# mLSTM branch operands by token chunks, the last gate unit's chunks in turns, and ada units moved ahead, in a one-core encoder step

## The chip, the core and the metric

The kernel runs on one core of a Trainium2 chip. The metric is the device time of one execution in microseconds, of which several runs are taken. The engines are named as in the profile: PE (TensorE matmul), PEld (its weight loads), DVE (VectorE), ACT (ScalarE), POOL (GpSimd), SP (SyncE, which here issues most DMAs).

## The reference, cut to what matters

One layer of an encoder for 1024 prompt tokens and one group of 64 sample tokens, so T = 1088 tokens, D_MODEL = 1024. Two branches, attention `y_a` and mLSTM `y_b`, are each projected to D_MODEL, weighted by sigmoid gates computed from the input, and summed.

```
mod = jax.nn.silu(c) @ w_ada + b_ada
sh1, sc1, g1, sh2, sc2, g2 = jnp.split(mod[:, None, :], 6, axis=-1)
u = _rmsnorm(x, norm1_g) * (1 + sc1) + sh1
proj = u @ w_in
sq, sk, sv, mqk_pre, mv, mo, mi, mf, ga, gb = jnp.split(proj, idx, axis=-1)
...
y_a = _stick_breaking(sq.reshape(B, L, SB_HEADS, SB_HEAD_DIM), k_all, v_all, q_start)
...
h, C1, n1, m1 = _mlstm(mq, mk, mvh, log_i, log_f, C0, n0, m0)
...
y_b = jax.nn.sigmoid(mo) * h
merged = jax.nn.sigmoid(ga) * (y_a @ w_a) + jax.nn.sigmoid(gb) * (y_b @ w_b)
x = x + g1 * (merged @ w_out)
u2 = _rmsnorm(x, norm2_g) * (1 + sc2) + sh2
x = x + g2 * ((jax.nn.silu(u2 @ w_ff_gate) * (u2 @ w_ff_up)) @ w_ff_down)
```

Attention has 8 heads of 64. For each block of 128 queries it takes the scores z, their sigmoid, a running product along the keys (as a scan), and the weighted sum of the values.

## The kernel before, in words

Everything is float32, and nearly every projection is made of three matmuls on operands split into a high and a low part (`mm3`, L75: high × high, high × low, low × high). Activations lie transposed, features on the 128 partitions and the 1088 tokens along the free axis, in three token chunks `CHUNKS` of 320, 384 and 384. A weight unit is 512 KB: its raw tile (`wr`, 3 buffers) is loaded from SP's queue, and POOL makes the high and the low tile out of it (`wh`, `wl`, 3 buffers each; L53 and L59).

The kernel is built by a scheduler that fixes the order of the instructions on each engine at build time: it reads the code as a list, and lets later work go ahead where it reckons an engine free. On the chip each engine then keeps that order, and waits on semaphores.

The part that the change touches is the phase "at", about 500 to 897 us of the profile. There four pairs of heads go through attention. `run(attention(p), chain(fill), 27, 0)` (L854) lists the whole of attention of pair p and behind it the dense filler; the scheduler weaves the filler in among attention's chains, which go from PE (scores, `z`, L526 and L527) over DVE (mask L388), ACT (sigmoid L392, `be` L393), DVE (scan L396, product `be` L397), back to PE (transposes into `ps_a`, L540), ACT and DVE (split into `ah` and `al`, L47 and L56), PE (`po`, L547), ACT and DVE (`yo`, `ya`, L553 and L554). Names read so: `be_3_0_5` is pair 3, head 0, query block 5.

The filler of pairs 0 to 2 is 14 gate units and 22 ada units. A gate unit (`gate_unit`, `unit` L346) projects the input (operands `uh`, `ul`, 8 feature blocks each) to 128 gate columns: for each chunk 24 matmuls over the 8 feature blocks kb into one PSUM bank, a sigmoid on ACT (L825), and a store from SP to `ga_d` or `gb_d`. `gb7` is the last of them, and the last reader of `uh` and `ul`. An ada unit (`ada_unit`, `ada_blocks` L213) loads 512 KB of w_ada into a `wr` buffer and makes 128 columns of the modulation: 16 small matmuls (L223), a copy on DVE (L226), a transpose on PE (L228), a sum and an addition on DVE (L233, L235).

The filler of pair 3 is 8 ada units (40 to 47) and then `branch_b` (L982): the mLSTM branch's projection by w_b. Its operands `yh4` to `yh7` and `yl4` to `yl7` lie ready split in DRAM (`yb_d`), and are loaded into the 16 buffers that held `uh` and `ul` (`load_y` with b of 4 or more, L963). Each of its 8 output blocks m takes the three chunks in turn: 12 matmuls into one of two banks (`cur["d"]` is 2), a load of the gate chunk `lgb` (L995), a copy on ACT (`tb`, L997), a multiply on POOL (L998), and a store to `pb_d` (L999). At m of 2, 3 and 4 it also loads attention's results of pairs 0 to 2 (`load_y(0)` to `load_y(2)`) and POOL splits them into `yh0` to `yl2`. The merge with w_a follows from 897 us, then w_out and the feed-forward part.

Of the kernel before, what the change touches and what calls it, by code (L numbers as in the profile page):

```python
# [8 lines left out]
F32 = mybir.dt.float32  # L9
# [5 lines left out]
P = 128  # L15
# [4 lines left out]
KB = 8  # L20
EPS = 1e-6
CHUNKS = [(0, 320), (320, 704), (704, 1088)]
# [13 lines left out]
def trunk(ctx, tc, a, o, dbg=None, stop=None):  # L36
    nc = tc.nc
# [14 lines left out]
    def hi_pool(out, in_):  # L52
        nc.gpsimd.tensor_scalar(out, in_, 1.0, 0.0, ALU.mult, ALU.add)  # L53
# [4 lines left out]
    def lo_pool(out, in_, h):  # L58
        nc.gpsimd.tensor_sub(out, in_, h.bitcast(F32))  # L59

    def w_unit(fills, name):
        raw = wp.tile([P, KB, P], F32, tag="wr", name=f"wr_{name}")
        for dst, src in fills(raw):
            nc.sync.dma_start(dst, src)
        wh = wp.tile([P, KB, P], F32R, tag="wh", name=f"wh_{name}")
        wl = wp.tile([P, KB, P], F32R, tag="wl", name=f"wl_{name}")
        hi_pool(wh, raw)
        lo_pool(wl, raw, wh)
        return wh, wl

    def cols(w, c0, n=P):

        return w[:, c0 : c0 + n].rearrange("(kb p) n -> p kb n", p=P)

    def mm3(ps, wh, wl, xh, xl, first, last):  # L75
        nc.tensor.matmul(ps, wh, xh, start=first, stop=False)  # L76
        nc.tensor.matmul(ps, wh, xl, start=False, stop=False)
        nc.tensor.matmul(ps, wl, xh, start=False, stop=last)
# [14 lines left out]
    w_a, w_b, w_out = a["w_a"][0], a["w_b"][0], a["w_out"][0]  # L93
# [50 lines left out]
    yb_d = dram.tile([4, 2, P, T], F32, name="yb_d")  # L144
# [37 lines left out]
    def small(shape, name, tag, dtype=F32, bufs=2, pool=None):  # L182
        return (pool or cur["sb"]).tile(shape, dtype, tag=tag, name=name, bufs=bufs)
# [11 lines left out]
    def bank(tag, name, bufs=2):  # L195
        return cur["ps"].tile([P, 512], F32, tag=tag, name=name, bufs=bufs)

    cur = {}
# [40 lines left out]
    uh, ul = [], []  # L239
# [11 lines left out]
    c0 = small([16, P], "c0", "c0", bufs=1)  # L251
# [91 lines left out]
    def evac_v(p, ps, s, e):  # L343
        nc.scalar.copy(pairs[p].vf[:, s:e], ps[:, : e - s])

    def unit(name, fills, evac, alloc=None):  # L346
        wh, wl = w_unit(fills, name)
        if alloc:
            alloc()
        for c, (s, e) in enumerate(CHUNKS):  # L350
            ps = bank("d", f"ps_{name}_{c}", cur["d"])
            for kb in range(KB):
                mm3(ps[:, : e - s], wh[:, kb, :], wl[:, kb, :], uh[kb][:, s:e], ul[kb][:, s:e], kb == 0, kb == KB - 1)
            evac(ps, s, e)
            yield

    def w_cols(c0):
        return lambda raw: [(raw, cols(w_in, c0))]
# [463 lines left out]
    def gate_unit(b, c0, dst, name):  # L822
        def fin(ps, s, e):
            t = small([P, 384], f"gt_{name}{b}_{s}", "gt", bufs=cur["gt"])
            nc.scalar.activation(t[:, : e - s], ps[:, : e - s], AF.Sigmoid)  # L825
            nc.sync.dma_start(dst[b][:, s:e], t[:, : e - s])
        return unit(f"{name}{b}", w_cols(c0 + b * P), fin)

    def in_unit(name, c0, i, evac, alloc):
        return unit(name, w_cols(c0), lambda ps, s, e: evac(*i, ps, s, e), lambda: alloc(*i))  # L830
# [12 lines left out]
    def ada_unit(i):  # L843
        ada_blocks((i,), "d", cur["d"], lambda i: wp.tile([P, KB, P], F32, tag="wr", name=f"wada{i}"))
        if 32 <= i < 40:
            b = i - 32
            nc.vector.tensor_scalar(A2[:, b, :], mod[:, i, :], 1.0, n2g(b), ALU.add, ALU.mult)
        yield

    def chain(gens):  # L850
        for g in gens:
            yield from g

    def run(consumer, dense, nsteps, nd):  # L854

        n = 0.0
        done = False
        if nd == 0:
            for _ in consumer:
                pass  # L860
            done = True
        for _ in dense:
            n += nsteps / max(nd, 1)
            while n >= 1.0 and not done:
                n -= 1.0
                done = next(consumer, "end") == "end"
        for _ in consumer:
            pass

    gates = [gate_unit(b, OFF_GA, ga_d, "ga") for b in range(KB)] + [gate_unit(b, OFF_GB, gb_d, "gb") for b in range(KB)]  # L870
    ada_left = [ada_unit(i) for i in range(16, 48)]
# [39 lines left out]
    for h in range(4):  # L911
        craw = small([P, P], f"c0_{h}", "S")
        nc.sync.dma_start(craw, a["state_mlstm_C"][0, 0, h])
        ps = bank("t", f"ps_c0{h}", 3)
# [24 lines left out]
    ps = bank("t", "ps_cvo", 3)  # L939
# [18 lines left out]
    yh, yl = {}, {}  # L958

    def y_tiles(b):  # L960
        yh[b] = up.tile([P, T], F32R, tag="u", name=f"yh{b}")
        yl[b] = up.tile([P, T], F32R, tag="u", name=f"yl{b}")

    def load_y(b):
        y_tiles(b)
        if b >= 4:
            for i, t in enumerate((yh[b], yl[b])):
                nc.sync.dma_start(t.bitcast(F32), yb_d[b - 4, i])
            return
        raw = up.tile([P, T], F32, tag="u", name=f"yr{b}")  # L970
        nc.sync.dma_start(raw, ya_d[b])
        for s, e in CHUNKS:
            hi_pool(yh[b][:, s:e], raw[:, s:e])
            lo_pool(yl[b][:, s:e], raw[:, s:e], yh[b][:, s:e])

    def wide_unit(w, r0, nb, q, name):

        ws = w_unit(lambda raw: [(raw.rearrange("p (k b) n -> p k (b n)", b=2)[:, :nb, :],
                                  w[r0 : r0 + nb * P, q * 256 : (q + 1) * 256].rearrange("(k p) n -> p k n", p=P))], name)
        return [x.rearrange("p (k b) n -> p k b n", b=2) for x in ws]  # L980

    def branch_b():  # L982

        for m in range(KB):
            if m % 2 == 0:
                wh, wl = wb0 if m == 0 else wide_unit(w_b, 0, 4, m // 2, f"wb{m}")
            if 2 <= m < 5:
                load_y(m - 2)
            for c, (s, e) in enumerate(CHUNKS):
                n = e - s  # L990
                ps = bank("d", f"ps_b{m}_{c}", cur["d"])
                for k in range(4):
                    mm3(ps[:, :n], wh[:, k, m % 2, :], wl[:, k, m % 2, :], yh[4 + k][:, s:e], yl[4 + k][:, s:e], k == 0, k == 3)
                gt = small([P, 384], f"lgb{m}_{c}", "gt", bufs=4)[:, :n]
                nc.sync.dma_start(gt, gb_d[m][:, s:e])  # L995
                t = small([P, 384], f"tb{m}_{c}", "gt", bufs=4)[:, :n]
                nc.scalar.copy(t, ps[:, :n])  # L997
                nc.gpsimd.tensor_mul(t, t, gt)  # L998
                nc.sync.dma_start(pb_d[m][:, s:e], t)  # L999
                yield  # L1000

    gi, ai = 2, 2
    for p, (ng, na) in enumerate(((5, 6), (5, 8), (4, 8))):
        gs, ads = gates[gi : gi + ng], ada_left[ai : ai + na]
        gi, ai = gi + ng, ai + na
        fill = []
        for i in range(na):
            fill += gs[i : i + 1] + ads[i * na // ng : (i + 1) * na // ng]
        run(attention(p), chain(fill), 27, 0)
    wb0 = wide_unit(w_b, 0, 4, 0, "wb0")  # L1010
    for b in range(4, 8):
        load_y(b)
    run(attention(3), chain(ada_left[24:32] + [branch_b()]), 27, 0)
    ph.close()


# [8 lines left out]
    def dbank(name):  # L1025
        return cur["p2"].tile([P, 512], F32, tag="d", name=name, bufs=6)
# [13 lines left out]
    for m in range(KB):  # L1040
        if m % 2 == 0:
            wh, wl = wide_unit(w_a, 0, 4, m // 2, f"wa{m}")
        for c, (s, e) in enumerate(CHUNKS):
# [6 lines left out]
            ps = dbank(f"ps_a{m}_{c}")  # L1050
# [224 lines left out]
    gb = gst.enter_context(tc.tile_pool(name="gb", bufs=8, space=PSUM, reuse_waits="tile"))  # L1275
# [243 lines left out]
    def add_x1(m, h, r, src):  # L1519

        if h is None:
            nc.vector.scalar_tensor_tensor(xq[m][:, :, r], src, gain(m, 0), xq[m][:, :, r], ALU.mult, ALU.add)
            return
        x = xq[m][:, h, r]
        for lo, hi, g in (by_group(0, QT) if h == r == 0 else [(0, QT, 0)]):
            nc.vector.scalar_tensor_tensor(x[:, lo:hi], src[:, lo:hi], gain(m, g), x[:, lo:hi], ALU.mult, ALU.add)
# [16 lines left out]
    def evac(p, m, h, ps):  # L1543
        if p == 5:
            add_x1(m, h, 1, ps)
        if p == 1:
            nc.scalar.copy(us[m][:, h], ps)
        elif p == 6:
            nc.vector.tensor_sub(us[m][:, h], us[m][:, h], ps)
            if h:  # L1550
                add_x1(m, None, 1, us[m])
                add_x1(m + 4, None, 1, us[m])
                for i in range(2):
                    add_x1(m + 4, i, 0, us[m][:, i])
        else:
            m_, r = {2: (m, 0), 5: (m + 4, 1), 3: (m, 1), 7: (m + 4, 1), 4: (m + 4, 0)}[p]
            add_x1(m_, h, r, ps)
            if p == 4:
                norm_step(m_, r, h)
            elif p != 5 and h:  # L1560
                norm_step(m_, r)
# [165 lines left out]
```

## Time and profile before

| | us |
|---|---|
| three runs | 1803.46, 1794.51, 1791.31 |
| median of the runs | 1794.51 |
| the profiled execution | 1791.73 |
| its span in the profile | 1790.0 |
| mean granted clock of PE | 0.988 |

The profile shows one execution; the times of its engines and stretches add up to its span, and a shift in them is set against 1791.73 us. The page's second part cuts the span into 40 slices of 44.75 us with the busy share in tenths (9 is 90% or more); the phase "at" is the twelfth to the twentieth of them:

```profile
PE   5899999999999999989998999999999999999998
```

A slice says little of what waits for what; for that the views by stretch and by wait are read, which the next sections quote.

### The profile page before, as it was taken

What the parts mean: (1) busy time and instruction counts of PE and PEld (TensorE: products, weight loads), DVE (VectorE), ACT (ScalarE), POOL (GpSimd) and SP (SyncE); (2) the same over time, 40 slices, a digit from 0 to 9 for tenths busy, and PEclk for the clock granted to TensorE, in tenths of its full rate; (3) what the DMA queues carried; (4) which work ended last, traced back from release to release, by engine and by line L of the source; (5) the groups of instructions that cost most, each with busy time, mean ns of one, the idle gap of its engine ahead of it and who ended that gap; (6) DMA issues with size and microseconds to landing.
All of it is one profiled execution on the core that took longest, in us unless ns stands there. A gap on an engine that the chain in (4) does not pass through costs nothing. (4 is left out here: it accounts for less than half of the span.)

```text
span 1790.0 us, 32786 instructions
## 1 busy us (share of the span) xinstructions
PE 1718.5 (96%) x12670; PEld 1656.9 (93%) x12670; DVE 1052.6 (59%) x2024; ACT 735.2 (41%) x1500; POOL 563.0 (31%) x507
## 2 busy tenths in 40 slices
PE   5899999999999999989998999999999999999998
PEld 4699999999988989877898999999999999999998
DVE  6623415152346858597554289666655677667965
ACT  5332333324233535353412367433333355453444
POOL 3434534545442232224877250044322100001000
PEclk9999999999999999999999999999999999999999
DMA  9426666664485565586576345744433488899852
GB/s 275 116 78 199 146 200 138 198 168 143 123 210 137 141 155 149 135 252 206 169 221 188 109 139 153 210 157 149 136 116 98 142 250 229 287 337 347 292 159 101
DMA packets 359533, 320.25 MB, mean 179 GB/s; under 512 B 16726, under 2 KB 327506, under 8 KB 359378
## 3 DMA queue, kind: packets, MB, share of 16 engines
q1 hardware_dynamic: 345074, 270.77, 50.2%
q0 software_dynamic: 14304, 47.39, 10.7%
q8 instruction: 100, 1.64, 0.4%
q14 instruction: 55, 0.45, 0.1%
HBM read 241.01 MB, written 98.09 MB: 189 GB/s over the span
## 5 line engine op out<-in xcount | busy, mean ns | idle before, releaser
L1609 PE MATMUL ps_d<-o,wh_d 128*128 128x272 f32 x1232 | 230.9, 287 | 0.2 <-DVE g L1370 0.2
L1609 PEld LDWEIGHTS ps_d<-o,wh_d 128*128 128x128 f32 x1232 | 192.9, 188 | 0.4 <-DVE g L1370 0.4
L1609 PE MATMUL ps_d<-o,wl_d 128*128 128x272 f32 x616 | 176.4, 288 | 0.0
L1609 PEld LDWEIGHTS ps_d<-o,wl_d 128*128 128x128 f32 x616 | 115.6, 188 | 0.0
L396 DVE TENSOR_TENSOR_SCAN re<-re 128x128 f32<-128x128 f32 (+3 forms) x64 | 105.8, 1654 | 14.3 <-ACT re L392 13.6
L47 ACT CAST w<-wr 128x512 fp32r<-128x512 f32 x140 | 85.0, 619 | 68.4 <-PE ps_gc L1382 27.1
L56 DVE TENSOR_TENSOR w<-wr,w 128x512 fp32r<-128x512 f32 x140 | 94.9, 691 | 21.4 <-ACT w L47 17.6
L1593 POOL DMA_DIRECT2D dsum_d<-wr_d x12 | 6.5, 538 | 237.9 <-DVE wr_d L1591 232.0
L392 ACT ACTIVATE re<-z 128x512 f32<-128x512 f32 (+2 forms) x96 | 47.5, 495 | 75.3 <-DVE z L388 55.4
L1382 PE MATMUL ps_ga<-b1h,w 128*128 128x272 f32 x352 | 74.6, 289 | 3.0 <-ACT g L1367 1.9
L1382 PE MATMUL ps_gc<-b5h,w 128*128 128x272 f32 x352 | 75.1, 293 | 0.0
L1382 PE MATMUL ps_gb<-b6h,w 128*128 128x272 f32 x352 | 74.4, 289 | 0.0
L1382 PE MATMUL ps_gd<-b7h,w 128*128 128x272 f32 x352 | 74.1, 290 | 0.2 <-DVE hst L1374 0.2
L1382 PE MATMUL ps_gd<-b4h,w 128*128 128x272 f32 x352 | 73.8, 289 | 0.4 <-DVE hst L1364 0.4
L1382 PE MATMUL ps_ga<-b2h,w 128*128 128x272 f32 x352 | 73.8, 288 | 0.0
L1382 PE MATMUL ps_gc<-b3h,w 128*128 128x272 f32 x352 | 73.7, 289 | 0.0
L47 ACT CAST o<-hr 128x544 fp32r<-128x544 f32 x77 | 49.0, 645 | 49.9 <-DMA hr<-h_d 23.9
L47 ACT CAST wh_d<-wr_d 128x1024 fp32r<-128x1024 f32 (+1 forms) x42 | 41.2, 981 | 66.6 <-PE ps_d L1609 26.6
L76 PE MATMUL ps_ga<-uh,wh_ga 128*128 128x384 f32 (+1 forms) x192 | 65.1, 339 | 3.4 <-ACT gt_ga L825 3.3
L56 DVE TENSOR_TENSOR o<-hr,o 128x544 fp32r<-128x544 f32 x77 | 53.9, 723 | 21.0 <-ACT o L47 20.6
L76 PE MATMUL ps_gb<-uh,wh_gb 128*128 128x384 f32 (+1 forms) x192 | 65.1, 339 | 0.0
L56 DVE TENSOR_TENSOR al<-ps_a,ah 128x512 fp32r<-128x512 f32 (+1 forms) x80 | 49.3, 631 | 25.7 <-ACT ah L47 25.3
(550 smaller groups left out, 5891.9 us busy)
## 6 DMA issues: line engine op xcount, KB each, us to landing
wada<-in_w_ada SPq DMA_DIRECT2D x48, 512.0 KB
wr<-wsum_d SPq DMA_DIRECT2D x80, 256.0 KB
wr_d<-in_w_ff_down SPq DMA_DIRECT2D x34, 512.0 KB
h_d<-hst SPq DMA_DIRECT2D x44, 272.0 KB
wr<-in_w_ff_gate SPq DMA_DIRECT2D x40, 256.0 KB
hr<-h_d SPq DMA_DIRECT2D x33, 272.0 KB
wsum_d<-in_w_ff_up POOLq DMA_DIRECT2D x6, 1282.0 KB, 7.6
wsum_d<-in_w_ff_gate POOLq DMA_DIRECT2D x6, 1282.0 KB, 7.9
```

The costliest lines, as they stand in the source:

```text
L47: nc.scalar.copy(out, in_)
L56: nc.vector.tensor_sub(out, in_, h.bitcast(F32))
L76: nc.tensor.matmul(ps, wh, xh, start=first, stop=False)
L392: nc.scalar.activation(rest[:, c0 : c0 + w], ps, AF.Sigmoid, scale=-scale)
L396: nc.vector.tensor_tensor_scan(r, r, r, 1.0, ALU.mult, ALU.bypass)
L1382: nc.tensor.matmul(ps, w[:, a, j, :], b[j // 2][:, j % 2, :], start=p in (1, 6, 5, 7) and j == 0 and k == 0, stop=j == 3 and k == 2, skip_ ...
L1593: nc.gpsimd.dma_start(dsum_d[p][mp, ks[0] // 4][:, : P * n], flat)
L1609: nc.tensor.matmul(ps, a[:, j, mi, :], b[:, h], start=p not in (2, 4) and k == ks[0] and i == 0, stop=k == ks[-1] and i == 2, skip_group_c ...
```

## The change: what it does

Four things.

1. `unit` gets a flag `last`, set for `gb7`: its chunk 0 goes as before, then chunks 1 and 2 are written with the feature blocks kb as the outer loop, both banks held at once, both evacuated at the end.
2. The loads of `yh4` to `yl7` from `yb_d` are cut by token chunk: 24 DMAs of 160 or 192 KB (three chunks, four heads, high and low) instead of 8 of 544 KB. The tiles are all taken first. `load_y` loses its branch for b of 4 or more.
3. `branch_b` goes by two groups of four output blocks, and in each group chunk by chunk: chunk 0 of blocks 0 to 3, then chunk 1, then chunk 2. Two weight units are therefore held at a time. `load_y(0)` to `load_y(2)` stand at its 7th, 10th and 13th step; before they stood ahead of its 7th, 10th and 13th step too.
4. The 8 ada units of pair 3 move into the filler of pairs 0 to 2, which then have 8, 11 and 11 ada units instead of 6, 8 and 8. Pair 3's filler is `branch_b` alone.

```diff
-    def unit(name, fills, evac, alloc=None):
+    def unit(name, fills, evac, alloc=None, last=False):
...
         for c, (s, e) in enumerate(CHUNKS):
+            if last and c:
+                break
...
             evac(ps, s, e)
+            yield
+        if last:
+            pss = [bank("d", f"ps_{name}_{c}", cur["d"]) for c in (1, 2)]
+            for kb in range(KB):
+                for ps, (s, e) in zip(pss, CHUNKS[1:]):
+                    mm3(ps[:, : e - s], wh[:, kb, :], wl[:, kb, :], uh[kb][:, s:e], ul[kb][:, s:e], kb == 0, kb == KB - 1)
+            for ps, (s, e) in zip(pss, CHUNKS[1:]):
+                evac(ps, s, e)
             yield
...
-        return unit(f"{name}{b}", w_cols(c0 + b * P), fin)
+        return unit(f"{name}{b}", w_cols(c0 + b * P), fin, None, name == "gb" and b == KB - 1)
...
         y_tiles(b)
-        if b >= 4:
-            for i, t in enumerate((yh[b], yl[b])):
-                nc.sync.dma_start(t.bitcast(F32), yb_d[b - 4, i])
-            return
...
-        for m in range(KB):
-            if m % 2 == 0:
-                wh, wl = wb0 if m == 0 else wide_unit(w_b, 0, 4, m // 2, f"wb{m}")
-            if 2 <= m < 5:
-                load_y(m - 2)
-            for c, (s, e) in enumerate(CHUNKS):
+        left = 3
+        for m4 in range(0, KB, 4):
+            wbs = [wb0 if m == 0 else wide_unit(w_b, 0, 4, m // 2, f"wb{m}") for m in (m4, m4 + 2)]
+            for i, (c, m) in enumerate((c, m4 + i) for c in range(3) for i in range(4)):
+                (s, e), (wh, wl) = CHUNKS[c], wbs[m % 4 // 2]
+                if left and (m4 or i >= 6) and i % 3 == 0:
+                    load_y(3 - left)
+                    left -= 1
...
-    for p, (ng, na) in enumerate(((5, 6), (5, 8), (4, 8))):
+    for p, (ng, na) in enumerate(((5, 8), (5, 11), (4, 11))):
...
     for b in range(4, 8):
-        load_y(b)
-    run(attention(3), chain(ada_left[24:32] + [branch_b()]), 27, 0)
+        y_tiles(b)
+    for s, e in CHUNKS:
+        for b in range(4, 8):
+            for i, t in enumerate((yh[b], yl[b])):
+                nc.sync.dma_start(t[:, s:e].bitcast(F32), yb_d[b - 4, i, :, s:e])
+    run(attention(3), branch_b(), 27, 0)
```

What the scheduler makes of it is seen in the built order. The places follow. Each row has the line, the operation, the result with what it is made of, and the shape; the lines of the changed kernel are 11 to 13 higher here.

The first place is PE at the start of branch_b (`ps_b0_0` is its block 0, chunk 0). Before, the end of attention's head 0 of pair 3:

```order
L228 MATMUL ps_ada46_9031<-ident_66,ada_sb46_9042 128x128
L547 MATMUL po3_0_3_8545<-ah_3_0_3_6_8589,vs3_0_8323 128x256
L547 MATMUL po3_0_3_8545<-al_3_0_3_6_8590,vs3_0_8323 128x256
L547 MATMUL po3_0_3_8545<-ah_3_0_3_6_8589,vs3_0_8323 128x128
L547 MATMUL po3_0_3_8545<-al_3_0_3_6_8590,vs3_0_8323 128x128
L228 MATMUL ps_ada47_9047<-ident_66,ada_sb47_9058 128x128
L76 MATMUL ps_b0_0_9063<-yh4_8304,wh_wb0_8300 128x320
L77 MATMUL ps_b0_0_9063<-yl4_8305,wh_wb0_8300 128x320
```

Now, in the middle of that head, behind the transposes of `be_3_0_5`:

```order
L551 MATMUL ps_a3_0_2_2_8629<-ident_66,be_3_0_5_8606 128x128
L551 MATMUL ps_a3_0_2_2_8629<-ident_66,be_3_0_4_8590 128x128
L551 MATMUL ps_a3_0_2_2_8629<-ident_66,be_3_0_5_8606 128x128
L76 MATMUL ps_b0_0_9085<-yh4_8432,wh_wb0_8428 128x320
L77 MATMUL ps_b0_0_9085<-yl4_8433,wh_wb0_8428 128x320
L76 MATMUL ps_b1_0_9104<-yh4_8432,wh_wb0_8428 128x320
L77 MATMUL ps_b1_0_9104<-yl4_8433,wh_wb0_8428 128x320
L537 MATMUL z3_0_7_512_8676<-kh3_0_8465,qs3_0_8464 128x512
```

branch_b's first matmuls now stand ahead of the last scores of head 0 of pair 3; before, the stretch from gb7's end to them held 130 attention rows and ten ada units, with no other work.

The second place is PE at the last gate unit. Before, `gb7` stands behind the transposes of query block 3 of the pair before:

```order
L540 MATMUL ps_a2_1_1_2_7625<-ident_66,be_2_1_2_7593 128x128
L540 MATMUL ps_a2_1_1_2_7625<-ident_66,be_2_1_3_7604 128x128 x2
L76 MATMUL ps_gb7_0_8180<-uh0_125,wh_gb7_8176 128x320
L77 MATMUL ps_gb7_0_8180<-ul0_126,wh_gb7_8176 128x320
L78 MATMUL ps_gb7_0_8180<-uh0_125,wl_gb7_8177 128x320
```

Now it stands behind those of block 7, and later its chunk 1 goes through all blocks before chunk 2 takes up `uh0`:

```order
L551 MATMUL ps_a2_1_3_2_7845<-ident_66,be_2_1_6_7806 128x128
L551 MATMUL ps_a2_1_3_2_7845<-ident_66,be_2_1_7_7822 128x128
L76 MATMUL ps_gb7_0_8294<-uh0_125,wh_gb7_8290 128x320
L77 MATMUL ps_gb7_0_8294<-ul0_126,wh_gb7_8290 128x320
L76 MATMUL ps_gb7_1_8322<-uh0_125,wh_gb7_8290 128x384
L77 MATMUL ps_gb7_1_8322<-ul0_126,wh_gb7_8290 128x384
```

```order
L76 MATMUL ps_gb7_1_8322<-uh7_139,wh_gb7_8290 128x384
L558 MATMUL po2_1_3_7831<-al_2_1_3_6_7876,vs2_1_7295 128x256
L558 MATMUL po2_1_3_7831<-ah_2_1_3_6_7875,vs2_1_7295 128x128
L558 MATMUL po2_1_3_7831<-al_2_1_3_6_7876,vs2_1_7295 128x128
L76 MATMUL ps_gb7_2_8323<-uh0_125,wh_gb7_8290 128x384
L77 MATMUL ps_gb7_2_8323<-ul0_126,wh_gb7_8290 128x384
```

So `gb7` comes four query blocks of attention later, and of the turns only the first two matmuls of chunk 1 and the last few of both chunks are woven.

The third place is SP's queue at the loads of `yh4` to `yl7` and of branch_b's first weight unit (`wr_wb0`). Before:

```order
L64 DMA wr_wb0_8298<-in_w_b 128x4x256
L220 DMA wada40_8936<-in_w_ada 128x8x128
L826 DMA gb_d_97<-gt_gb7_0_8205 128x320
L968 DMA yh4_8304<-yb_d_95 128x1088
L826 DMA gb_d_97<-gt_gb7_320_8233 128x384
L968 DMA yl4_8305<-yb_d_95 128x1088
```

Now, at the end of the loads of chunk 0:

```order
L1025 DMA yl7_8439<-yb_d_95 128x320
L837 DMA gb_d_97<-gt_gb7_320_8372 128x384
L837 DMA gb_d_97<-gt_gb7_704_8375 128x384
L1025 DMA yh4_8432<-yb_d_95 128x384
L1025 DMA yl4_8433<-yb_d_95 128x384
L64 DMA wr_wb0_8426<-in_w_b 128x4x256
L1025 DMA yh5_8434<-yb_d_95 128x384
L1025 DMA yl5_8435<-yb_d_95 128x384
```

`wr_wb0` stood ahead of all these loads and stands behind ten of them, and `wr_wb2` behind all twenty-four.

## The prediction

> **What bounds the kernel now.** I read the page's busy times first, then the busy time of each engine in stretches, then the waits of PE in the same stretches, then PE's, DVE's, POOL's and SP's timelines around the one stretch that the change rewrites.
>
> ```profile
> PE 1718.5 (96%) x12670; PEld 1656.9 (93%) x12670; DVE 1052.6 (59%) x2024; ACT 735.2 (41%) x1500; POOL 563.0 (31%) x507
> ```
>
> The span is 1790.0 us, so PE idles 71.5 us in all: matmul work is the bound, and the change neither adds nor removes a matmul. Only PE's idle time, and the clock at which it runs, can move. The stretches (columns: stretch, length, then busy us and instructions of PE, PEld, DVE, ACT, POOL, then granted clock, DMA share, GB/s):
>
> ```profile
> 500.00:772.00 272.00, 262.07 (x1865) 241.63 (x1864) 188.34 (x366) 120.61 (x283) 80.96 (x85) 0.98 0.62 153
> 785.30:824.70 39.40, 31.34 (x310) 23.50 (x309) 32.43 (x81) 20.07 (x45) 3.41 (x3) 0.96 0.95 288
> 812.00:819.00 7.00, 5.39 (x51) 4.03 (x52) 4.83 (x14) 1.46 (x4) 0.00 (x0) 0.76 0.71 193
> 876.00:884.00 8.00, 5.11 (x25) 4.67 (x24) 2.52 (x5) 2.60 (x6) 8.00 (x10) 0.79 0.40 122
> ```
>
> 500 to 772 is attention of pairs 0 to 2 with its filler: 9.9 us idle in 272. 785.3 to 824.7 is the weak place: the filler has run out (gb7, the last gate unit, has ended, branch_b has not begun), attention runs alone beside ten ada units, and PE idles 8.06 of 39.4 us. PE's own waits, first in 500 to 772, then in 785 to 826, then in 826 to 897:
>
> ```profile
> PE ps_a L540 <- DVE be L397: 3.1, 4, 1.5
> PE po L547 <- DVE al L56: 2.7, 2, 1.5
> PE ps_ys L509 <- DVE ys L507: 2.3, 1, 2.3
> PE ps_a L540 <- DVE ya L511: 1.6, 2, 1.1
> ...
> PE ps_ada L223 <- DMA wada<-in_w_ada: 2.9, 1, 2.9
> PE ps_ada L228 <- DVE ada_sb L226: 2.1, 1, 2.1
> PE po L547 <- DVE al L56: 1.4, 1, 1.4
> PE ps_a L540 <- DVE be L397: 1.3, 2, 0.8
> PE z L526 <- ACT be L393: 0.4, 1, 0.4
> ...
> PE ps_b L76 <- ACT tb L997: 3.1, 2, 2.6
> ```
>
> The first four sum to 9.7, the next five to 8.1. Nearly all are attention's own chain on DVE. No wait names the operands of branch_b: its first matmul stands behind the last attention row and starts without one.
>
> ```profile
> 824.56 0.29 PE L228 MATMUL ps_ada<-ident,ada_sb 128*128 128x128 f32 x1
> 824.66 0.38 PE L76 MATMUL ps_b<-yh,wh_wb 128*128 128x320 f32 x1
> ```
>
> So the fixed order on PE, not the landing of yh and yl, keeps branch_b until 824.66.
>
> **The change part by part.** The sum is made against the profiled execution's 1791.73 us; the median of the runs, 1794.51, lies 2.8 above it.
>
> A, branch_b starts inside attention of pair 3. Its first matmuls stand behind be_3_0_5's transposes instead of behind all of head 3_0; the long gap's 130 attention rows no longer stand together. Its 8.1 us of waits go, and with them the slow clock at 812 to 819: 7 us at 0.76 cost 7 × 0.24 = 1.7. Together −9.8. The Trainium skill ("TensorE: Matmul & The Clock Gate", What's actually happening) says that the clock falls after an idle window of about 3.4 us; the longest wait quoted above is 2.9, and 0.76 was granted all the same. By that rule the 1.7 would not hang on these waits, and A would be −8.1; the measured row decides.
>
> B, new gaps in its place. The order after has four filler-free stretches around gb7 and the first chunk of branch_b: 47, 42, 30 and 14 attention rows, 133 together, as many as before. Six ada units (42 to 47) still lie in them. In 500 to 772 attention alone waited 9.7 us over the 138 rows of its six gaps, 0.070 a row. 133 × 0.070 = +9.3. A second way, by engines: the long gap had 32.43 us of DVE in 39.4, a share of 0.82.
>
> ```profile
> 809.42 0.28 DVE L226 COPY ada_sb<-ps_ada 128x128 f32<-128x128 f32 x1
> 809.62 0.16 DVE L233 TENSOR_REDUCE mod<-ps_ada 128x2 f32<-128x8 f32 x1
> 809.81 0.16 DVE L235 TENSOR_TENSOR mod<-mod,c1T 128x2 f32<-128x2 f32 x1
> ...
> L223 PE MATMUL ps_ada<-wada,cT 128*32 128x128 f32 x160 | 8.9, 300 | 2.9 <-DMA wada<-in_w_ada 2.9
> L228 PE MATMUL ps_ada<-ident,ada_sb 128*128 128x128 f32 x10 | 3.0, 299 | 2.1 <-DVE ada_sb L226 2.1
> ```
>
> An ada costs DVE 0.60 us; without ten of them 26.4 us of DVE stay, 32 us at that share, against 31.34 − 8.9 − 3.0 = 19.4 to 22 us of PE: 10 to 13 us of waiting, less what the interleaved chunk of branch_b covers. Ends: 3.1, the long gap's waits on DVE's al and be and on ACT alone (1.4 + 1.3 + 0.4); 13. I take 9.3, which the mid gaps' rows show directly.
>
> C, eight more ada units in pairs 0 to 2. PE's and DVE's work only moves. But the gates now meet more ada between them, and the order of the mid stretch has eight gaps with 190 attention rows where it had six with 138. 52 × 0.070 = +3.7; per gap it would be 2 × 9.7 / 6 = 3.2. Ends 0 and 3.7; I take +3.4. The 8 × 512 KB of weights go into a stretch at a DMA share of 0.62: 4.2 MB over 272 us is 15 GB/s beside 153, hidden.
>
> D, the tail of branch_b. PE waited 2.6 us for a tb copy there, behind POOL, which was busy all of 876 to 884, and the clock of 0.79 cost 8 × 0.21 = 1.7.
>
> ```profile
> 865.72 3.81 POOL L53 TENSOR_SCALAR yh<-yr 128x320 fp32r<-128x320 f32 x3
> ...
> 879.97 0.64 PE L76 MATMUL ps_b<-yh,wh_wb 128*128 128x320 f32 x1 [2.60 <-ACT tb L997]
> ...
> 896.14 2.82 POOL L59 TENSOR_TENSOR yl<-yr,yh 128x320 fp32r<-128x320 f32 x3
> ```
>
> After, POOL's splits of yh0 to yl2 stand more evenly among the tb multiplies: yh0, yl0 and yh1 followed one another without one, now a tb multiply stands between the parts of yl0, and again behind yh1. The same POOL work must still end before ps_a can use yl2. Ends −4.3 (wait and clock gone) and 0 (moved to ps_a's wait for yl2). I take −3.0, nearer the row that shows the wait, since the order takes away its cause.
>
> E, the loads by chunk: 24 instead of 8, and wr_wb0 and wr_wb2 stand behind ten and twenty-four of them on SP.
>
> ```profile
> 780.21 0.34 SPq L968 DMA_DIRECT2D yh<-yb_d  x1
> ...
> 782.28 0.75 SPq L968 DMA_DIRECT2D yl<-yb_d  x1
> ...
> 818.34 5.27 SPq L64 DMA_DIRECT2D wr_wb<-in_w_b  x3
> ...
> 821.76 1.04 POOL L53 TENSOR_SCALAR wh_wb<-wr_wb 128x1024 fp32r<-128x1024 f32 x1 [25.79 <-DMA wr_wb<-in_w_b]
> 822.88 2.37 POOL L59 TENSOR_TENSOR wl_wb<-wr_wb,wh_wb 128x1024 fp32r<-128x1024 f32 x1
> ```
>
> Issue costs SP 0.34 to 0.75 us each. The 8 × 544 KB and two units of 512 KB are 5.5 MB: at the long gap's 288 GB/s 19.1 us from the first load's issue, then wh_wb2 1.04, a tb multiply of about 1.0 and wl_wb2 2.37: 23.5 us. PE needs wl_wb2 in row 4434 of its order, 89 attention and ada rows and 58 matmuls of branch_b and gb7 after the first load may go. An attention instruction took (39.4 − 8.9 − 3.0) / 140 = 0.20 us there with its waits; an instruction of the mid stretch 262.07 / 1865 = 0.14. That is 17.8 + 8.1 = 25.9 us: covered by 2.4. If the loads go at SP's slowest pace (24 × 0.75 = 18.0, then 3.4 from issue to split, 4.4 of splits and a gb chunk's landing of 3.1, which tb0_0 ahead of wl_wb2 needs) it is 28.9, late by 3.0.
>
> ```profile
> 830.83 0.43 SPq L995 DMA_DIRECT2D lgb<-gb_d  x1
> ...
> 833.94 1.01 POOL L998 TENSOR_TENSOR tb<-tb,lgb 128x384 f32<-128x384 f32 x1 [1.22 <-DMA lgb<-gb_d]
> ```
>
> (830.83 to 833.94 is that 3.1.) I take 0 and keep +3.0.
>
> F, chunks 1 and 2 of gb7 in turns. In the built order chunk 1 runs on to block 7 before chunk 2 takes up uh0, since chunk 2 waits for chunk 0's bank; only two matmuls at each end interleave. uh0 still comes free in the last chunk, as before. 0; nothing of E's start moves.
>
> Sum: −9.8 + 9.3 + 3.4 − 3.0 + 0 + 0 = −0.1, so 1791.6 of 1791.73; I say 1792. The long gap isn't closed, it is cut in four.
>
> **The rivals.** (1) A gain: chunk 0 of branch_b and gb7 cover attention so well that only B's low end is left, the mid gaps cost nothing more, and the tail's wait and clock go wholly: −9.8 + 3.1 + 0 − 4.3 = −11.0, so 1781. For it: DVE works ahead while PE does filler. Against: the mid stretch has filler too and waits in every gap.
>
> (2) Slower: gb7 arrives late. Its weight load waits on SP until ada42's matmuls give back a buffer, and on POOL its split stands behind six loads of head 3_1, which wait for the scores of head 2_1. From ada42's last matmul: 3.4 to land, six issues on POOL, 3.4 of splits, against 39 attention rows at 0.20 = 7.8 us and two adas.
>
> ```profile
> 795.41 0.56 POOL L438 DMA_DIRECT2D vs<-v_d  x1 [13.70 <-PE ps_ada L228]
> ...
> qs<-qk_d POOLq DMA_DIRECT2D x2, 272.0 KB, 8.2
> ```
>
> Six issues at 0.56 are 3.4, in all 10.2 beside some 9 to 12: it decides once POOL must also wait for an earlier one of those loads to land, 8.2 us. Then PE stands at ps_gb7_0 for that time: 1791.6 + 8.2 = 1800. Against it: before, the same loads of POOL stalled nothing on PE.
>
> (3) The turns do what they say, and uh0 comes free a chunk earlier. The order speaks against it, and since the old loads were not waited for, the price is 0 either way: 1792.
>
> (4) Small loads run one behind another. 24 × 2.7 (between 2.3, from 833.39 to 835.73, and 3.1) is 65 us, less the 25.9 covered: +39, 1831. Against it: before, seven loads were issued within 5.2 us and overlapped.
>
> ```profile
> 785.41 0.40 SPq L968 DMA_DIRECT2D yh<-yb_d  x1
> ...
> 833.39 0.32 SPq L995 DMA_DIRECT2D lgb<-gb_d  x1
> ...
> 835.73 0.88 POOL L998 TENSOR_TENSOR tb<-tb,lgb 128x320 f32<-128x320 f32 x1 [0.78 <-DMA lgb<-gb_d]
> ```
>
> The Trainium skill ("DMA: Bandwidth & Descriptors", Bandwidth) asks for DMAs of 1 MiB or more, and its Anatomy of one DMA gives each a fixed cost of about 2.0 us; its fit, for another issuing path, would make about 2.4 us of such a chunk, an estimate that agrees with the 2.3 to 3.1 seen. It speaks against cutting the loads, yet overlapping ones hide that cost here.
>
> **How the numbers follow.** Forecast (with rival 3, same time) 0.54; rival 1 0.20; rival 2 0.19; rival 4 0.03; the rest 0.04 for mixtures outside. The range reaches from rival 1, 1781, to rival 2 with E's end, 1800 + 3.0, and a microsecond for the runs' spread: 1781 to 1804. A measurement of this kernel tells about 1% (18 us) from no change. Faster by that would need 18 of the 8.1 + 1.7 + 9.7 + 4.3 = 23.8 us of idle time and slow clock counted above: 0.04. Slower by that needs rival 4, or rival 2 with every bad end: 0.05. Within: 0.91.
>
> **What would show it.** A: no stretch at 0.76 with filler-free attention of 39 us, branch_b some 15 us earlier relative to head 3_0. B: PE waits on be, al or ada_sb just ahead of gb7 and of ps_b0_0, 9 us in all; under 4 is rival 1. C: 500 to 772's waits at 13 rather than 9.7. D: no 2.6 us at a tb copy. E: ps_b waits named wl_wb or yh. Rival 2: ps_gb7 waits for POOL's wh_gb or wl_gb. I am wrong if PE's order on the chip leaves a wait that none of these name.

## The result and the profile after

The changed kernel is slower: its four runs have a median of 1817.92 us (1815.38 to 1827.5) against 1797.25 us (1791.31 to 1803.46) for the kernel before, a ratio of 1.0126 with a 95% interval of 1.0105 to 1.0148. The forecast was 1792, with 1804 as the upper end.

First, the busy times of the engines in the profile of the changed kernel, whose span is 1818.0 us:

```profile
PE 1728.6 (95%) x12670; PEld 1664.1 (92%) x12670; DVE 1042.6 (57%) x2024; ACT 734.9 (40%) x1500; POOL 567.3 (31%) x507
```

PE still carries the time, with the same 12670 matmuls. It idles 89.4 us instead of 71.5 and is busy 10.1 us longer for the same work, so both more waiting and a slower clock are to be looked for. The profiles differ by 28.0 us: 5.3 before attention starts (the end of the mLSTM heads comes at 487.0 before and 492.3 after, and between 487.5 and 491.5 in the experiments' profiles below), 18.8 from there to the first matmul of the output projection, 3.9 behind. Only the middle part holds the change. Here are its whole length and its last piece, the merge, in the view of busy times by stretch (stretch, length, busy us and instructions of PE, PEld, DVE, ACT, POOL, granted clock, DMA share, GB/s); first the kernel before:

```profile
487.00:945.20 458.20, 431.22 (x3009) 399.13 (x3010) 306.40 (x578) 190.33 (x447) 193.23 (x185) 0.98 0.66 178
896.50:945.20 48.70, 48.20 (x292) 47.66 (x291) 27.49 (x43) 10.15 (x26) 35.80 (x31) 1.00 0.74 223
```

The changed kernel, first pieces of the part and in the last row the whole of it, which is the same work:

```profile
505.30:785.90 280.60, 261.37 (x1888) 238.36 (x1887) 180.08 (x379) 121.38 (x282) 81.59 (x84) 0.96 0.61 154
785.90:846.00 60.10, 48.88 (x359) 41.39 (x357) 46.66 (x83) 26.52 (x59) 19.10 (x14) 0.91 0.77 214
610.00:620.00 10.00, 5.53 (x32) 4.23 (x33) 5.48 (x12) 2.91 (x6) 0.00 (x0) 0.66 0.41 98
760.00:770.00 10.00, 5.11 (x37) 3.96 (x37) 6.60 (x23) 3.75 (x11) 3.40 (x2) 0.80 1.05 221
800.00:810.00 10.00, 6.88 (x34) 5.76 (x34) 9.64 (x20) 3.41 (x7) 1.76 (x1) 0.66 1.01 193
914.60:969.30 54.70, 49.18 (x291) 47.70 (x290) 29.31 (x47) 10.95 (x28) 38.98 (x32) 1.00 0.69 207
492.30:969.30 477.00, 435.75 (x3009) 400.45 (x3009) 298.50 (x577) 191.76 (x447) 199.86 (x186) 0.97 0.63 171
```

Idle time of PE over the whole part is length less busy: 27.0 us before, 41.3 after, +14.3; the other 4.5 of the 18.8 is the same work taking longer, at a clock of 0.97 instead of 0.98. The first row is the nearest counterpart of 500 to 772 of the prediction, attention of pairs 0 to 2 with its filler: 19.2 us idle in place of 9.9, and a clock of 0.96 in place of 0.98. The three rows of 10 us show where that clock is: at places where PE also idles for 3.1 to 4.9 us. PE's waits, in 505 to 786, then 786 to 846, then 846 to 969 (who waits, for whom, us in all, how often, longest):

```profile
PE po L558 <- DVE al L56: 5.1, 2, 4.8
PE ps_gb L76 <- POOL wh_gb L53: 4.1, 1, 4.1
PE ps_a L551 <- DVE be L408: 3.3, 3, 1.4
PE z L537 <- DMA kh<-qk_d: 2.2, 1, 2.2
PE ps_ga L76 <- DVE mod L233: 1.4, 1, 1.4
PE ps_gb L78 <- POOL wl_gb L59: 1.0, 1, 1.0
...
PE ps_ada L228 <- DVE ada_sb L226: 2.9, 2, 2.5
PE z L537 <- ACT be L404: 2.8, 1, 2.8
PE ps_b L78 <- POOL wl_wb L59: 2.6, 1, 2.6
...
PE ps_b L76 <- POOL wh_wb L53: 0.8, 1, 0.8
...
PE ps_a L76 <- DVE lga L1066: 5.5, 4, 2.0
PE ps_b L76 <- ACT tb L1006: 2.6, 2, 2.3
```

Two sorts are new. Gates, and then branch_b's first unit, wait for their split weights (`wh_gb`, `wl_gb`, `wl_wb`). Single waits have a length that attention's own chain did not give before (4.8 on `al`). And the tail's wait for `tb` is still there, with 5.5 us of the merge's waits for `lga` beside it.

The wait for `wh_gb` can be followed back through the timelines of PE, SP, POOL and PE again. It is the seventh of the gb gates, gb6, which stands behind three ada units:

```profile
757.95 0.42 PE L223 MATMUL ps_ada<-wada,cT 128*32 128x128 f32 x6
...
758.42 0.38 SPq L64 DMA_DIRECT2D wr_gb<-in_w_in  x1
...
766.48 1.04 POOL L53 TENSOR_SCALAR wh_gb<-wr_gb 128x1024 fp32r<-128x1024 f32 x1 [7.92 <-DMA wr_gb<-in_w_in]
...
767.58 0.63 PE L76 MATMUL ps_gb<-uh,wh_gb 128*128 128x320 f32 x1 [4.07 <-POOL wh_gb L53]
```

The last six matmuls of the first of those three ada units start at 757.95; within half a microsecond SP issues the gate's load. The built order says why: this load waits for the matmuls of ada39, the first of the three, and ada39 stands behind gb5. It is ready for the split 8 us later, at a DMA share of 1.05 (the loads of the next ada units go beside it), and PE has by then run out of other work. In the kernel before, gb6's load waits for a matmul too, but for that of ada33, which stands ahead of gb5. So it could go a whole gate earlier, and its split began 18 us ahead of gb6's first matmul, where it now begins 1.1 us ahead:

```profile
723.09 0.38 SPq L64 DMA_DIRECT2D wr_gb<-in_w_in  x1
...
729.09 1.04 POOL L53 TENSOR_SCALAR wh_gb<-wr_gb 128x1024 fp32r<-128x1024 f32 x1 [7.96 <-DMA wr_gb<-in_w_in]
...
747.04 0.42 PE L76 MATMUL ps_gb<-uh,wh_gb 128*128 128x320 f32 x1
```

In the built order of the changed kernel this holds for each unit behind three ada units (gb4, gb6, gb7 and branch_b's `wb0`): its load waits for the first of the three.

The wait of 4.8 us on `al` hangs on DVE, which stood at the cast of q for the sample tokens, and that on a load that POOL issued late and that then took long:

```profile
595.78 1.32 POOL L53 TENSOR_SCALAR wh_gb<-wr_gb 128x1024 fp32r<-128x1024 f32 x1 [12.58 <-DMA wr_gb<-in_w_in]
...
601.42 0.54 POOL L446 DMA_DIRECT2D qs<-qk_d  x1
...
613.62 0.20 DVE L487 CAST zq<-qs 128x64 fp32r<-128x64 f32 x1 [6.51 <-DMA qs<-qk_d]
...
614.47 0.58 PE L558 MATMUL po<-al,vs 128*128 128x256 f32 x1 [4.82 <-DVE al L56]
```

In the kernel before, counted from the end of the heads (487.0, and 492.3 after), POOL came to the same gate's split 6.0 us sooner and to the same load 2.3 us sooner, and DVE waited 0.17 us there:

```profile
584.52 2.42 POOL L53 TENSOR_SCALAR wh_gb<-wr_gb 128x1024 fp32r<-128x1024 f32 x1 [7.22 <-DMA wr_gb<-in_w_in]
...
593.85 0.54 POOL L435 DMA_DIRECT2D qs<-qk_d  x1
...
602.07 0.20 DVE L476 CAST zq<-qs 128x64 fp32r<-128x64 f32 x1 [0.17 <-DMA qs<-qk_d]
```

So one queue that works in order (POOL) hands the lateness of a gate's weights to attention, and a second one (DVE) hands it on to PE. That is the smaller part of it: the cast came 6.3 us later, of which the late issue is 2.3. The rest is the load itself, which with its twin took 9.8 to 11.1 us from issue to landing, against 5.6 to 7.1 before; why isn't shown (SP had issued an ada unit's weights at 600.40, 1.0 us ahead of it).

### The profile page after: what moved, and what is told of

It is laid out like the page before. It is cut to its first block, busy times and chain, and to the rows that moved or that the text cites. A ratio compares the mean times of both kernels' runs of the same rounds, so it can differ in the third digit from the quotient of the medians.

```text
span 1818.0 us, 32782 instructions
## 1 busy us (share of the span) xinstructions
PE 1728.6 (95%) x12670; PEld 1664.1 (92%) x12670; DVE 1042.6 (57%) x2024; ACT 734.9 (40%) x1500; POOL 567.3 (31%) x507
## 5 line engine op out<-in xcount | busy, mean ns | idle before, releaser
L407 DVE TENSOR_TENSOR_SCAN re<-re 128x128 f32<-128x128 f32 (+3 forms) x64 | 98.2, 1537 | 9.8 <-ACT re L403 9.3
```

The costliest lines, as they stand in the source:

```text
L407: nc.vector.tensor_tensor_scan(r, r, r, 1.0, ALU.mult, ALU.bypass)
```

## The experiments

Four theories were held against each other; the expectations call them M (later W), B, D and S. M, later W: the moved ada units make the gates' weights late, since both take their raw tiles from the three buffers of `wr`. B: the reordered branch_b with its loads by chunk costs. D: the ada units cost by their own work on DVE and by their hold on the two PSUM banks. S: any edit makes the scheduler shuffle the order, and no part carries the loss. Every edit also makes the scheduler order other instructions anew, so no run changes one thing alone, and the controls below matter. Each time and ratio is set against runs of the kernel before that were made with it.

**The parts alone.** The ada move alone, on the kernel before:

```diff
-    for p, (ng, na) in enumerate(((5, 6), (5, 8), (4, 8))):
+    for p, (ng, na) in enumerate(((5, 8), (5, 11), (4, 11))):
...
-    run(attention(3), chain(ada_left[24:32] + [branch_b()]), 27, 0)
+    run(attention(3), branch_b(), 27, 0)
```

> The kernel before with the 8 ada units of pair 3 moved into pairs 0 to 2 (8, 11 and 11), nothing else changed. Theory M (the moved ada units cost: each takes one of three weight buffers, so gate weights arrive later, and the loads and splits behind them on POOL too): most of the 21 us by which the median grew, so 1805 to 1818, with PE waits on POOL's splits and DVE waits on loads of qs in pairs 1 and 2. Theory B (the reordered branch_b with loads by chunk costs): 1797 or below, since pair 3 loses ten ada units' waits. Theory S (every new list makes the scheduler shuffle the order, and no part carries the loss): somewhere between 1790 and 1810, with waits at other places than in the changed kernel.

It took 1809.71 us against 1795.89, a ratio of 1.0075 (1.0049 to 1.0101). Its waits are those of the changed kernel, at the same places of the order:

```profile
611.22 0.58 PE L547 MATMUL po<-al,vs 128*128 128x256 f32 x1 [4.63 <-DVE al L56]
...
761.42 0.64 PE L76 MATMUL ps_gb<-uh,wh_gb 128*128 128x320 f32 x1 [4.24 <-POOL wh_gb L53]
```

The opposite, all of the change but the ada move:

```diff
-    for p, (ng, na) in enumerate(((5, 8), (5, 11), (4, 11))):
+    for p, (ng, na) in enumerate(((5, 6), (5, 8), (4, 8))):
...
-    run(attention(3), branch_b(), 27, 0)
+    run(attention(3), chain(ada_left[24:32] + [branch_b()]), 27, 0)
```

> The changed kernel with the ada units back in their pairs (6, 8, 8 and 8 in pair 3 ahead of branch_b). M: 1792 to 1800, no wait of PE at gb7 for POOL and no 6 us wait of DVE for qs. B: 1810 to 1820. S: between.

1800.45 us, ratio 1.0021 (1.0000 to 1.0042). The loads by chunk with the new branch_b, without the turns in gb7 (the diff is that of `branch_b` and of the loads, as shown with the change):

> The kernel before with loads by token chunk and branch_b by groups of four blocks, without the turns in gb7 and without the moved ada units. M: 1792 to 1800. B: 1808 to 1818, with the tail's tb waits and the waits of ps_a for lga that the changed kernel shows. S: between.

1800.34 us, ratio 1.0024 (1.0007 to 1.0041). The turns alone (the diff is that of `unit` and `gate_unit`):

> The kernel before with gb7's chunks 1 and 2 written in turns, nothing else. M and B: 1794 to 1800, no change. S: off by up to 10 either way, since even this small edit changes the list that the scheduler reads.

1798.43 us, ratio 1.0013 (0.9993 to 1.0033): no change that can be told. So the ada move carries 13.8 of the 20.7 us, the new branch_b some 4, the turns nothing that can be told. The rest of some 2 us is within the intervals. M was right and B wrong, though 1800.45 and 1800.34 lie just above M's upper end of 1800 for these two kernels.

The 4 us were halved once more. Loads by chunk with the old branch_b (the diff of the loads alone):

> The kernel before with the mLSTM operands loaded in 24 DMAs by token chunk instead of 8, branch_b unchanged. If the loads carry the 4 us that both e2 and e3 lost: 1797 to 1801, with a PE wait at ps_b for yh or for a split. If the order of branch_b carries them: 1792 to 1797.

1798.69 us, ratio 1.0009 (0.9994 to 1.0025). The new branch_b with whole loads (the diff of `branch_b` alone):

> The kernel before with branch_b by groups of four blocks, its operands still loaded whole. If the order carries the 4 us: 1797 to 1801, with the merge's waits on lga that the changed kernel shows. If the loads carry them: 1792 to 1797.

1799.82 us, ratio 1.0015 (0.9995 to 1.0036). Neither is told from no change, so this split stays undecided. The profile of the loads and branch_b together shows the waits of the merge for `lga`, in 870 to 951 us; that of branch_b alone has 3.5 us of them, that of the loads alone none:

```profile
PE ps_a L76 <- DVE lga L1059: 3.1, 2, 2.0
```

**Supply or work.** Now the changed kernel with the ada units' raw weights in turns among three sets of buffers; nothing is computed otherwise:

```diff
-        ada_blocks((i,), "d", cur["d"], lambda i: wp.tile([P, KB, P], F32, tag="wr", name=f"wada{i}"))
+        ada_blocks((i,), "d", cur["d"], lambda i: wp.tile([P, KB, P], F32, tag=("wr", "wh", "wl")[i % 3] if i >= 18 else "wr", name=f"wada{i}"))
```

> The changed kernel, but the ada units' raw weights take turns among the three buffers each of wr, wh and wl instead of wr alone; the bytes, the instructions and the memory stay the same. Theory W (supply: three ada units between two gates use up wr's three buffers, so that the next gate's weights can be loaded only when an ada's matmuls on PE are done, and POOL, which works in order, keeps splits and loads of q and k waiting behind them): 1797 to 1808, no PE wait for wh_gb at gb7, no 6 us wait of DVE for qs. Theory D (the ada units' own work in a stage where DVE is 70% busy, and the two PSUM banks that they share with the gates): 1814 to 1822, the same PE waits for mod, ada_sb and be. Theory S (shuffled order): anything, with waits elsewhere.

1798.76 us against 1794.26: the ratio falls from 1.0126 to 1.0035 (1.0020 to 1.0050). All waits of a gate for POOL are gone, and the 4.8 us on `al` is 0.7 (the wait that this expectation and a later one place at gb7 is the one at gb6). What is left in 505 to 786 us is of D's sort, attention and banks:

```profile
PE ps_a L551 <- DVE be L408: 4.7, 4, 1.3
PE ps_as L498 <- DVE be_s L408: 2.7, 1, 2.7
PE ps_ada L228 <- DVE ada_sb L226: 2.5, 2, 2.3
...
PE ps_gb L76 <- DVE mod L233: 1.5, 1, 1.5
...
PE po L558 <- DVE al L56: 0.7, 1, 0.7
```

It is not little: all the waits of this window sum to 17.2 us, against 19.0 in the changed kernel. The gain shows behind it, in 786 to 846, where PE idles 3.5 us at full clock instead of 11.2 at 0.91 (these 60 us hold more matmuls, 399 against 359), and in the whole part, 463.3 us instead of 477.0:

```profile
786.00:846.00 60.00, 56.54 (x399) 51.97 (x398) 48.12 (x78) 28.70 (x66) 25.87 (x22) 1.00 0.75 226
490.50:953.80 463.30, 433.04 (x3009) 400.20 (x3009) 319.07 (x584) 193.55 (x451) 206.59 (x189) 0.97 0.65 177
```

The same edit on the ada move alone and, as a control, on the kernel before:

> The kernel before with the moved ada units alone, and their weights in turns among wr, wh and wl. W: 1792 to 1801. D: 1807 to 1813. S: between.

1803.55 us, ratio 1.0059 (1.0039 to 1.0079): its interval overlaps that of the ada move on `wr`, so a gain isn't shown here. W's number was missed; the result lies between W and D, where S had put it.

> The kernel before with the ada weights in turns among wr, wh and wl, as a control. W: 1788 to 1798, little to gain since before there are at most two ada units between gates; perhaps the 2.9 us wait of an ada in pair 3 for its weights goes. D: 1794 to 1799. S: off by up to 8.

1802.05 us, ratio 1.0052 (1.0034 to 1.0070): the turns cost some 8 us where little was to be gained. W's and D's numbers were missed here, and S's range holds it. That price may be why the run before it gained so little. Waits of ada units for DVE's copy grew to 9.2 us in 505 to 958 of that profile; why the turns bring them was not followed further.

```profile
PE ps_ada L228 <- DVE ada_sb L226: 9.2, 6, 3.2
```

The control says that an edit which relieves nothing can move the time by about 0.5%; a single result of 8 us does not prove W. A proof has to be larger, or tied to a place. Two ada units behind each gate, two left in pair 3:

```diff
-    for p, (ng, na) in enumerate(((5, 8), (5, 11), (4, 11))):
+    for p, (ng, na) in enumerate(((5, 10), (5, 10), (4, 8))):
...
-    run(attention(3), branch_b(), 27, 0)
+    run(attention(3), chain(ada_left[30:32] + [branch_b()]), 27, 0)
```

> The changed kernel with 28 ada units in pairs 0 to 2, two behind each of the 14 gates, and the last two at the start of pair 3: six of the eight are still moved, but no gate has three ahead of it. W: 1800 to 1808. D: 1812 to 1818 (six eighths of the moved work stay). S: anything between 1795 and 1820.

1804.21 us, ratio 1.0062 (1.0042 to 1.0082): by the ratios some 12 us come back although six of the eight units are still moved. W's range, not D's (S allowed it too). Then the clumps without the move: the kernel before, every ada unit in its old pair, but in threes behind every other gate:

```diff
-            fill += gs[i : i + 1] + ads[i * na // ng : (i + 1) * na // ng]
+            fill += gs[i : i + 1] + ads[3 * ((i + 1) // 2) : 3 * ((i + 2) // 2)]
```

> The kernel before with the same ada units in the same pairs, but behind every other gate in clumps of three instead of one or two behind each. No work moves from one pair to another. W: three raw weights in a row use up wr's buffers: 1801 to 1812, with PE or DVE waits on POOL's splits or loads in pairs 0 to 2. D: 1791 to 1799, since DVE and the banks have the same work. S: up to 8 either way, and such waits are not tied to the clumps.

1830.42 us against 1796.58, ratio 1.0184 (1.0153 to 1.0214): 34 us slower with the same work in each pair, and far beyond every number expected, W's too. In its built order each gate behind three ada units loads only after the first of the three. D, which saw nothing here, falls as it was put; that a clump also holds the two PSUM banks longer is not excluded by this run. From the heads' end to the output projection, and its waits for POOL in 505 to 786 us:

```profile
490.50:986.00 495.50, 440.88 (x3009) 401.66 (x3009) 312.28 (x578) 192.43 (x447) 209.82 (x188) 0.96 0.62 165
...
PE ps_ga L76 <- POOL wh_ga L53: 4.3, 1, 4.3
...
PE ps_gb L76 <- POOL wh_gb L53: 2.3, 1, 2.3
PE ps_gb L78 <- POOL wl_gb L59: 2.1, 2, 1.3
```

The waits that name POOL are 8.7 us here, and 9.8 in the whole part, of 54.6 us idle. The waits for `be` and `al` have grown more: in the whole part the transposes wait 11.3 us for `be` and `po` 11.2 for `al`, against 4.7 and 4.9 in the kernel before. That these too come of late gates, since attention then stands without filler, is argued and not shown; the turns were not tried on this kernel.

**Tied to a place.** The turns in pair 2 alone (`if i >= 37` in the edit above):

> The changed kernel with the ada weights in turns among wr, wh and wl in pair 2 alone (units 37 to 47); pairs 0 and 1 keep wr. W: gb7's 4 us wait for POOL's wh_gb goes, with the waits behind it in pairs 2 and 3; the 4.8 us wait of PE near 614 us, behind DVE's wait for qs in pair 1, stays at its place: 1804 to 1813. D: 1814 to 1822, both stay. S: the wait in pair 1 isn't tied to the place of the edit and may go or stay.

1796.75 us, ratio 0.9997 (0.9980 to 1.0013): all of the loss is back, more than W expected (1804 to 1813). The clumps, their work and their PSUM banks are as in the changed kernel; only the buffers of their weights differ, and with them the built order, in which gb6 and gb7 now wait for no matmul. In its profile the part is 464.4 us long, against 477.0 and, before, 458.2, so this one execution shows two thirds of the gain there. The wait in pair 1 stays, as it said:

```profile
612.07 0.58 PE L558 MATMUL po<-al,vs 128*128 128x256 f32 x1 [3.34 <-DVE al L56]
```

And the clumps of pair 2 taken away with all units on `wr`, three of them now behind branch_b (the clump at the end of pair 1 stays):

```diff
-    for p, (ng, na) in enumerate(((5, 8), (5, 11), (4, 11))):
+    for p, (ng, na) in enumerate(((5, 8), (5, 11), (4, 8))):
...
-    run(attention(3), branch_b(), 27, 0)
+    run(attention(3), chain([branch_b()] + ada_left[29:32]), 27, 0)
```

> The changed kernel with three ada units taken out of pair 2 and put behind branch_b in pair 3: pair 2 has two units behind each gate and no clump of three, every ada unit uses wr as in the changed kernel, five of the eight are still moved. W: 1792 to 1801, as far down as the buffers in turns brought it. D: 1812 to 1818. S: between.

1798.21 us, ratio 1.0014 (0.9998 to 1.0029): the loss is gone without touching a buffer, in W's range. In the built order gb6 and gb7 wait again for ada units that stand ahead of the gate before them. The whole part is back at the length and idle time of the kernel before (458.2 and 27.0):

```profile
489.00:947.90 458.90, 432.05 (x3009) 398.43 (x3010) 296.46 (x577) 190.64 (x446) 196.65 (x186) 0.98 0.65 177
```

Its waits in 505 to 786 us name no split of POOL any more. The six rows are all that the view has there, and the wait on `al` in pair 1 is among them, where nothing was altered:

```profile
PE po L558 <- DVE al L56: 4.4, 3, 3.6
PE ps_ga L76 <- DVE mod L233: 2.7, 1, 2.7
PE z L537 <- DMA kh<-qk_d: 2.3, 1, 2.3
PE ps_ada L228 <- DVE ada_sb L226: 2.3, 2, 1.9
PE ps_gb L76 <- DVE mod L233: 1.6, 2, 0.8
PE ps_a L551 <- DVE be L408: 0.4, 1, 0.4
```

Last, the turns added to it:

> The same with the ada weights in turns among wr, wh and wl in pair 2 and behind branch_b. W: within 4 of the run before it, since without clumps the buffers have nothing left to give. If the turns help in a way of their own: 5 or more below it.

1807.51 us, ratio 1.0069 (1.0044 to 1.0094): some 10 us slower. Both expectations were missed; it is about the price that the control paid. In these two kernels, which have no clump in the pairs that the turns were to relieve, the turns cost 8 to 10 us; where that cost comes from is open.

No version of these was faster than the kernel before beyond its interval.

## Why the prediction was wrong

The step that failed is C, "eight more ada units in pairs 0 to 2": it was taken at +3.4 us with ends of 0 and 3.7. The stretch shows +9.3 us of idle time. It also has some 3 us more of slow clock: counting only what PE was busy at half clock, read in quarter-microsecond stretches, 8.4 us were lost there against 5.5 before. That is about +12. The ada move alone, with what it does to pair 3, gives +13.8. What was left out is the supply of weights. The working counted the ada units' matmuls, their DVE work and their bytes, and found each hidden; it counted attention rows per gap at the rate of the old gaps. It did not ask what buffer the next gate's load waits for once three ada units stand ahead of it. That the clumps in pair 2 make the loss is shown two ways: buffers in turns there, and no clumps there. The clumps on the old kernel, in all three pairs, show that clumps without the move cost as much and more.

The late gates' price did not all fall inside C's stretch. With the buffers in turns everywhere the part is 13.7 us shorter and idles 11.0 us less, most of that behind 786, while the stretch itself still waits 17.2 us, part of which may be the price of the turns. Without turns and without the clumps of pair 2 the waits of that window sum to 13.7, against C's 9.7 + 3.4 = 13.1. So the rate per row was not far off, with five of the eight units moved; the missing term was the supply.

The second rival held the mechanism, a gate that arrives late because its load waits for an ada's buffer, with POOL behind it. It saw it at gb7 only, priced one wait of 8.2 us, and got 0.19. On the chip it is gb6 that PE waits 4.1 us for, gates from then on run later against attention, and the whole came to more than 8.2. With 0.19 it was weighed far below the forecast's 0.54.

A and B: the long gap did go, and waits of about the expected size came in its place: 11.2 us idle in 785.9 to 846, where B's 9.3 was expected; 3.4 of it are waits for branch_b's split weights. But B had no clock term: PE lost 3.7 us there at half clock. So A and B together, less the 3.4, gave −9.8 + 7.8 + 3.7 = +1.7 instead of −0.5. That B's size came out is luck in part: with the buffers in turns the same 60 us idle 3.5 at full clock, so much of it were the late gates and not the gaps of which B was made.

E was taken at 0 with an end of +3.0: the waits for `wl_wb` and `wh_wb` are 2.6 + 0.8 = 3.4 us, just past its end. It was wb0 that was waited for, not wb2 as the working had it, and the loads by chunk are not the reason: no profile with these loads and the ada units in their old pairs has such a wait, and the ada move alone, with whole loads, has 0.8 us of it. In the built order wb0's load waits for the matmuls of ada45, the first unit behind gb7, where before it waited for ada37, ahead of gb7. So this seems to belong to the supply too: it is gone with the buffers in turns and with three units behind branch_b, but 1.3 us stay with two units behind each gate. The loads by chunk themselves cost nothing that can be told (1.0009), which was right. The Trainium skill ("DMA: Bandwidth & Descriptors", Bandwidth) asks for DMAs of 1 MiB or more; cutting 544 KB loads into 160 and 192 KB did not show here.

D was taken at −3.0. The wait for `tb` stayed, 2.6 us against 3.1, and the merge idles 54.70 − 49.18 = 5.5 us where it idled 0.5: DVE's multiply by `lga` is late. D's ends, −4.3 and 0, did not hold this +5.0. The kernels with branch_b's new order and the ada units in their old pairs have 2.9 to 3.5 us of these waits, and those with the old order at most 0.5 (1.7 in the one with threes); but the kernels that keep the new order with buffers in turns, two units behind each gate or three behind branch_b have none, or 0.4. So the new order brings the waits only together with where the merge comes to stand; the cause stays open.

F, the turns in gb7, was right: no change that can be told (1.0013), as the built order undoes most of them. Rival 4, small loads one behind another, was excluded as said. The first rival's hope, gaps that are covered so that only 3.1 us remain, came true only behind 786 in the kernels with the buffers in turns (3.5).

## What to carry to other kernels

When a unit is moved in front of others that share its buffers, count how many units lie between two users of one buffer, and ask whose end the next load now waits for; work and bytes may both be hidden while the load is not. Here a gate with three units of the other sort between it and the gate before it could load only when that gate was done. A late filler can cost more than the wait that names it: gb6's wait was 4.1 us, and the loss that went with its clumps some 20. And before a gain of half a per cent is read as proof, run a control that carries the same edit where there is nothing to relieve: here such a control alone moved the time by 0.5%.

## What the runs showed of the hardware

Read in quarter-microsecond stretches, the granted clock of the part is 1.00 or 0.50 both before and after, with values between only where it changes. A mean of 0.66 over 10 us is thus a mixture. In the changed kernel it is 0.50 from about 612.4 to 619.1, around the end of the single wait of 4.82 us, and from about 800.2 to 806.9, where waits of 2.48 and 2.78 us stand with one transpose between them. In the kernel before it is 0.50 from about 814.8 to 818.1, behind waits of 2.13 and 0.81 us. Its price, estimated as half of PE's busy time at that clock, is 2.4, 2.0 and 1.7 us. The Trainium skill ("TensorE: Matmul & The Clock Gate", What's actually happening) lets the clock fall after an idle window of about 3.4 us; the first place, with a wait longer than that, agrees with it, the other two, with no single wait of that length, do not.
